# Layer-1 tables of the state-space branch: computed beside the layer-0 prompt attention instead of among the first projections

## The chip, the core and the metric

The kernel runs on one core of a Trainium2 chip. The metric is device time per execution in microseconds, as the median of the runs. Further numbers come from one execution that the hardware profiler recorded. The engines are TensorE (PE, matmuls; PEld is its weight loads), VectorE (DVE), ScalarE (ACT), GpSimd (POOL) and SyncE (SP, which issues all the DMAs here).

## What is computed

Two layers of a trunk with two parallel branches, for one prompt of 2048 tokens and eight samples of 16 tokens (each with 512 cached keys), width 1024. Cut from the reference:

```python
mod = silu(c) @ w_mod + b_mod                       # shift, scale, gate
h = rms_norm(x, norm_g) * (1 + scale) + shift
u, z_s, q, k, v, z_a = split(h @ w_in)              # each 512 wide
ab = exp((a_re + i a_im) * dt)                      # per group (32) and state (64)
bb = (ab - 1) / (a_re + i a_im) * b                 # input matrix
state_t = ab * state_{t-1} + bb @ u_t               # associative scan over time
y_s = Re(c @ state) + d_skip * u                    # then GELU and a half-GLU
z = q @ k.T / 8                                     # stick-breaking, s < t
a[t, s] = sigmoid(z[t, s]) * prod_{s<j<t} (1 - sigmoid(z[t, j]))
y_a = a @ v
x = x + gate * (concat(y_s * silu(z_s), y_a * silu(z_a)) @ w_out)
```

The state-space scan is not run token by token: chunks of 16 tokens are done by matmuls with matrices made of the powers of `ab`, and from chunk to chunk the state is carried by a scan in rotated coordinates. Those matrices and rotations depend on the weights alone. They are the tables that this document is about.

## The kernel before

Matmul operands of the projections are split into a high and a low part, so a product is three matmuls (hH wH, hH wL, hL wH). Tiles are 128 tokens; half 0 is tiles 0 to 7 and the samples' tile 16, half 1 is tiles 8 to 15. `build` (line 52 on) writes the work in this order: `mod` for layer 0 (conditioning), `ssm_params` (powers of `ab` for both layers, to DRAM), the projections of half 0 (`project`, first u and q, then k, v, za, zs), between them the tables, then half 1's projections with `ssm(0)` and `attn_sample(0)`, then `attn_prompt(0)`, `glu(0)`, the rest of `mod` (layer 0's gate and all of layer 1's), `output(0, 0)` (the output projection of half 0), and layer 1's projections.

The tables of a layer are made by two functions:

- `ssm_phase(l)` builds cos and sin of 128 chunk rotations by seven doublings. Each step multiplies on VectorE (lines 444, 447) and on GpSimd (445, 448) and joins on VectorE (446, 449); then `unit` normalises (ScalarE squares at 414 and 415, VectorE at 416 to 418, GpSimd at 419). The result T goes to DRAM (`ph_d`, 3 MB).
- `ssm_mats(l)` loads b, c and d, turns them by transposes on TensorE (497, 517), and makes in eight blocks of four groups EE (VectorE 551, GpSimd 550 and 552), GG (VectorE 556 and 557, GpSimd 555), KK (TensorE 563, ScalarE 566, VectorE 567) and mH (TensorE 573, ScalarE 576). The result goes to DRAM (`mm`, `kd`, `sm_d`; 10.5 MB).

`ssm(l)` and `ssm_sample(l)` read these tables from DRAM. Layer 0 needs its own early, in `ssm(0)`; layer 1 only in `ssm_sample(1)` and `ssm(1)`, which come after the layer-0 output.

`attn_prompt(l)` goes over blocks of four query tiles, pairs of heads and chunks of 512 keys. I call one such step a unit; layer 0 has 40, numbered from 0; the first chunk of each block and pair of heads is the masked one. In a unit TensorE makes scores (819, 820, and a mask at 822), ScalarE a sigmoid (824), VectorE a running product (826, shown as TENSOR_TENSOR_SCAN in the profile and as SCALAR_TENSOR_TENSOR in the program's order), TensorE transposes that (836), VectorE and ScalarE copy the transposes (838, 839) and TensorE multiplies with v (842). Up to 16 products `u` are kept, so the scores run about two units ahead.

SBUF is handed out as stacks from two sides. A pool that is opened where a closed one lay waits, tile by tile, until that tile's last user is done. On the right lie, one after another, the tables' pools, `ssm`, the sample attention and the prompt attention; on the left the projections' pool, then those of `glu`, `mod` and `output`. PSUM has tags: m (projections, `mod` on the left, output), z and t (scores and transposes of the attention, tables).

No order is written out by hand. At build time a scheduler goes over the program with a model of the engines and fixes a static order for each engine and for SyncE's queue; where several instructions are ready, the one written earlier goes first. On the chip each engine takes its instructions in that order and waits by semaphore, so an instruction that isn't ready holds all behind it on its engine.

Of the kernel before, what the change touches and what calls it, by code (L numbers as in the profile page):

```python
# [44 lines left out]
class Trunk:  # L45
# [6 lines left out]
    def build(self):  # L52
        tc, nc = self.tc, self.nc
        with ExitStack() as es:
            self.dram = es.enter_context(tc.tile_pool(name="dram", bufs=1, space=DRAM))
            self.cp = self.pool(es, "const")
            self.pes = ExitStack()
            self.mb, self.zb, self.tb, self.ob = 2, 2, 2, 1
            self.ps = self.pes.enter_context(tc.tile_pool(name="ps", bufs=1, space=PSUM))
            self.scratch()  # L60
            self.consts()
            with ExitStack() as pe:
                with ExitStack() as px:
                    self.xp, self.xf = self.pool(px, "xp", right=True), []
                    self.rs0 = self.xp.tile([128, NT], F32, name="rs")
                    self.fetch(0)
                    self.fetch(1)
                    with ExitStack() as pv:
                        su = self.pool(pv, "sv", right=True)
                        self.mod(0, (2, 3, 0, 1))  # L70
                        self.ssm_params(su)
                    st = self.proj_open(pe, 0, 0)
                    with tc.high_priority(offset=300):
                        self.project(st, ("u",))
                self.project(st, ('q',))
                with ExitStack() as pq:
                    self.stats(self.pool(pq, "stats1", right=True), TILES[1])
                self.ssm_mats(0)
                with ExitStack() as ph:
                    self.ssm_phase(ph, 0)  # L80
                    self.ssm_phase(ph, 1)
                self.ssm_mats(1)
                self.ssm_sample(0)
                self.project(st, ('k', 'v', 'za', 'zs'))
                self.proj_half(st, 1)
                self.project(st, ("u",))
                self.ssm(0)
                self.attn_sample(0)
                self.project(st, ('zs', 'za', 'k', 'v', 'q'))
            self.attn_prompt(0, ((0, 4), (4, 4), (8, 4), (12, 4)))  # L90
            self.glu(0)
            self.mod(0, (4, 5), right=False)
            self.mod(1, (2, 3, 0, 1, 4, 5), right=False)
            self.output(0, 0)
            with ExitStack() as pe:
                st = self.proj_open(pe, 1, 0)
                self.project(st, ("u",))
                self.project(st, ('q', 'k', 'v', 'za', 'zs'))
            self.attn_sample(1)
            self.output(0, 1)  # L100
            with ExitStack() as pe:
                st = self.proj_open(pe, 1, 1)
                self.project(st, ("u",))
                self.ssm_sample(1)
                self.ssm(1)
                self.project(st, ('k', 'v', 'q', 'zs', 'za'))
            self.pes.close()
            self.ps = es.enter_context(tc.tile_pool(name="ps2", bufs=1, space=PSUM))
            self.mb, self.zb, self.tb, self.ob = 1, 3, 3, 1
            self.attn_prompt(1, ((0, 4), (4, 4), (8, 4)) + ((12, 2), (14, 2)))  # L110
            self.glu(1)
            self.output(1, 0)
            self.output(1, 1)
# [304 lines left out]
        v.tensor_mul(c, c, t1)  # L418
        gp.tensor_mul(s, s, t1)

    def ssm_phase(self, es, l):
        v, gp = self.nc.vector, self.nc.gpsimd
        su = self.pool(es, f"sp{l}", right=True)
        pu = su.tile([128, 3, 16], F32, name="pu")
        self.dma(pu, self.pb_d[l][:, 1])
        T = su.tile([128, 2, 16, 128], F32, name="T")
# [26 lines left out]
        v.tensor_scalar(t1, s, -1.0, None, ALU.mult)  # L453
        self.dma(self.ph_d[l][:, 2], t1)

    def ssm_mats(self, l):
        nc, A = self.nc, self.A
        v, gp, ident = nc.vector, nc.gpsimd, self.ident
        NG = 4
        with ExitStack() as es:  # L460
            su = self.pool(es, f"sm{l}", right=True)
            PWT = su.tile([128, 18, 2, G], F32, name="PWT")
            self.dma(PWT, self.pw_d[l])
            FT = PWT[:, 17]
# [27 lines left out]
            C2 = su.tile([128, G, C], F32, name="C2")  # L492
            C3 = su.tile([128, G, C], F32, name="C3")
            for src, dst in ((Cn, C2), (Cm, C3)):
                ps = self.pt()
                for a in range(4):
                    nc.tensor.transpose(ps[:, a * 128:(a + 1) * 128], src[:, a, :, :].rearrange("p r x -> p (r x)"), ident)
                pv = ps.rearrange("p (g c) -> p g c", c=C)
# [13 lines left out]
            v.tensor_copy(ZB[hi, 1, :, 1], pairs(Bb1)[hi, :, 1])  # L512
            BT = su.tile([128, 2, 512], F32, name="BT")
            for r in range(2):
                ps = self.pt()
                for qt in range(4):
                    nc.tensor.transpose(ps[:, qt * 128:(qt + 1) * 128],
                                        ZB[:, r, qt * 4:(qt + 1) * 4].rearrange("p q g c -> p (q g c)"), ident)
                nc.scalar.copy(BT[:, r, :], ps)
# [22 lines left out]
            for b in range(G // NG):  # L542
# [13 lines left out]
                v.tensor_mul(GG, pw(0, 16), Bb1[:, gs].unsqueeze(2).to_broadcast([128, NG, 16, C]))  # L556
                v.tensor_add(GG, GG, t2)
                self.dma(self.mm[l][:, gs, 256:512], EE[:, :, 1:17, :].rearrange("p g n c -> p g (n c)"))
                ps = self.pz()
                for g in range(NG):  # L560
                    go = b * NG + g
                    lh = Bb1[:, go:go + 2, :] if go < G - 1 else Bz
# [5 lines left out]
                self.dma(self.kd[l][gs].rearrange("g c l k -> (g c) (l k)")[:, 256:512], KK)  # L568
                mH = su.tile([128, 2, NG, 128], F32, name="mH", bufs=2)
                for hf in range(2):  # L570
                    ps = self.pt()
                    for j in range(NG):
                        nc.tensor.transpose(ps[:, j * 128:(j + 1) * 128],
                                            GG[:, j, 8 - hf * 8:16 - hf * 8, :].rearrange("p t c -> p (t c)"), ident)
# [707 lines left out]
```

## Time and profile before

| | us |
|---|---|
| median of 3 runs (lowest, highest) | 3268.61 (3263.90, 3268.92) |
| the profiled execution | 3266.1 |
| its span, first to last instruction | 3264.3 |
| TensorE busy in the span | 3019.6 (93%) |
| VectorE busy | 2228.8 (68%) |
| ScalarE busy | 1297.2 (40%) |
| GpSimd busy | 715.0 (22%) |
| mean granted clock of TensorE | 0.971 |

Times in the trace count from the span's first instruction. A busy time is the union of an engine's instructions in a stretch. Ends of matmuls are modelled, so a busy TensorE may still hold some slack; how far apart matmuls start shows what one costs. A wait is put down to the instruction whose semaphore came last. The stretches used below are: 296 to 616 (both layers' phase tables, layer 1's matrices, and the k, v, za and zs projections of half 0), 1061 to 1383 (the layer-0 attention from the end of unit 0 to the end of unit 17), 1383 to 1914 (units 18 to 39).

### The profile page before, as it was taken

How to read it: one execution, taken by the hardware profiler on the slowest of the kernel's cores; microseconds unless marked ns; L12 is line 12 of the kernel's file. 1: busy time of each engine (PE TensorE's matmuls, PEld its weight loads, DVE VectorE, ACT ScalarE, POOL GpSimd, SP SyncE). 2: the span in 40 equal slices, each digit the busy share in tenths (PEclk: the TensorE clock that was granted, in tenths of full speed). 3: DMA queues.
4: the chain of work that ended last, by engine and by line, in shares of the span. 5: the costliest groups of instructions: out<-in, count | busy, mean ns of one | idle time of the engine just before them, and what ended most of it. 6: DMA issues, size and time to landing. Idle time of an engine off the chain costs nothing. (4 is left out here: it accounts for less than half of the span.)

```text
span 3264.3 us, 47172 instructions
## 1 busy us (share of the span) xinstructions
PE 3019.6 (93%) x16902; PEld 2241.4 (69%) x16902; DVE 2228.8 (68%) x3885; ACT 1297.2 (40%) x2646; POOL 715.0 (22%) x468
## 2 busy tenths in 40 slices
PE   6978679899998999999999999989999899999998
PEld 4756577798767667667777785757789565666665
DVE  6699785667466776677895534376583989776865
ACT  5622225334342343465443324263343345343422
POOL 1155663102211022211021002222200202111210
PEclk8989899999999999999999999999999899999999
DMA  6645654565776974343344237437853846444642
GB/s 208 164 141 176 215 166 150 146 192 167 258 241 216 315 218 151 121 139 117 113 150 153 88 104 268 142 99 216 268 177 119 259 129 200 141 128 136 203 140 73
DMA packets 516100, 555.28 MB, mean 170 GB/s; under 512 B 87203, under 2 KB 369491, under 8 KB 515098
## 3 DMA queue, kind: packets, MB, share of 16 engines
q1 hardware_dynamic: 515866, 552.26, 53.9%
q8 instruction: 134, 2.20, 0.3%
q14 instruction: 100, 0.82, 0.1%
HBM read 378.12 MB, written 169.86 MB: 168 GB/s over the span
## 5 line engine op out<-in xcount | busy, mean ns | idle before, releaser
L826 DVE TENSOR_TENSOR_SCAN u<-u 128x512 f32<-128x512 f32 (+3 forms) x640 | 722.2, 1162 | 94.2 <-ACT u L824 90.7
L673 PE MATMUL pm<-wH,hH 128*128 128x512 f32 x1088 | 448.9, 414 | 38.4 <-ACT kn L760 18.9
L675 PE MATMUL pm<-wH,hL 128*128 128x512 f32 x1088 | 446.2, 410 | 10.6 <-POOL hL L649 6.0
L674 PE MATMUL pm<-wL,hH 128*128 128x512 f32 x1088 | 444.0, 408 | 9.9 <-DVE wL L172 8.0
L839 ACT COPY aT<-pt 128x512 f32<-128x512 f32 (+1 forms) x376 | 174.9, 469 | 595.3 <-PE pt L836 569.1
L836 PEld LDWEIGHTS pt<-ident,u 128*128 128x128 f32 x2176 | 242.1, 142 | 230.8 <-issue 194.1
L824 ACT ACTIVATE u<-pz 128x512 f32<-128x512 f32 (+3 forms) x640 | 320.7, 535 | 177.1 <-PE pz L822 61.3
L838 DVE COPY aT<-pt 128x512 f32<-128x512 f32 (+1 forms) x376 | 199.4, 533 | 253.8 <-PE pt L836 242.3
L836 PE MATMUL pt<-ident,u 128*128 128x128 f32 x2176 | 352.0, 285 | 12.9 <-DVE aT L838 9.3
L842 PE MATMUL po<-aT,V 128*64 128x512 f32 (+1 forms) x1504 | 317.7, 505 | 16.0 <-DVE aT L838 8.1
L819 PE MATMUL pz<-K,Q 128*128 128x512 f32 (+2 forms) x640 | 272.9, 427 | 6.1 <-ACT u L824 1.8
L726 PE MATMUL pm<-hH,wH 128*128 128x384 f32 (+1 forms) x768 | 258.9, 337 | 18.4 <-DVE kn L731 18.4
L673 PEld LDWEIGHTS pm<-wH,hH 128*128 128x128 f32 x1088 | 210.0, 193 | 90.2 <-ACT kn L760 20.4
L728 PE MATMUL pm<-hH,wL 128*128 128x384 f32 (+1 forms) x768 | 257.4, 336 | 10.2 <-POOL wL L172 10.2
L172 POOL TENSOR_TENSOR wL<-wr,wH 128x512 fp32r<-128x512 f32 x96 | 152.1, 1595 | 498.2 <-ACT wH L171 326.8
L727 PE MATMUL pm<-hL,wH 128*128 128x384 f32 (+1 forms) x768 | 257.8, 336 | 0.0
L675 PEld LDWEIGHTS pm<-wH,hL 128*128 128x128 f32 x1088 | 210.2, 193 | 66.2 <-POOL hL L649 10.6
L674 PEld LDWEIGHTS pm<-wL,hH 128*128 128x128 f32 x1088 | 210.2, 193 | 58.8 <-DVE wL L172 11.3
L820 PE MATMUL pz<-K,Q 128*128 128x512 f32 (+2 forms) x640 | 236.3, 370 | 0.0
L1241 PE MATMUL pm<-owH,mH 128*128 128x512 f32 x512 | 205.0, 402 | 2.1 <-ACT mH L171 1.2
L1242 PE MATMUL pm<-owL,mH 128*128 128x512 f32 x512 | 204.1, 399 | 3.1 <-DVE owL L172 3.1
L1243 PE MATMUL pm<-owH,mL 128*128 128x512 f32 x512 | 202.4, 396 | 0.0
(373 smaller groups left out, 5252.0 us busy)
## 6 DMA issues: line engine op xcount, KB each, us to landing
wr<-in_w_in_dram SPq DMA_DIRECT2D x192, 256.0 KB
K<-kT SPq DMA_DIRECT2D x184, 256.0 KB
Q<-qT SPq DMA_DIRECT2D x112, 256.0 KB
wm<-in_w_mod_dram SPq DMA_DIRECT2D x24, 1024.0 KB
V<-dv_d SPq DMA_DIRECT2D x92, 256.0 KB
out_dram<-kn SPq DMA_DIRECT2D x68, 256.0 KB
qT<-x SPq DMA_DIRECT2D x64, 256.0 KB
kT<-x SPq DMA_DIRECT2D x64, 256.0 KB
```

The lines of the kernel that those rows point to most:

```text
L673: pe.matmul(ps, hH[:, k, cs], wH[k], start=k == 0, stop=False)
L674: pe.matmul(ps, hH[:, k, cs], wL[k], start=False, stop=False)
L675: pe.matmul(ps, hL[:, k, cs], wH[k], start=False, stop=k == KT - 1)
L726: pe.matmul(ps[:, 0:n], wH[k][:, ws], hH[:, k, 0:n], start=k == 0, stop=False)
L727: pe.matmul(ps[:, 0:n], wH[k][:, ws], hL[:, k, 0:n], start=False, stop=False)
L728: pe.matmul(ps[:, 0:n], wL[k][:, ws], hH[:, k, 0:n], start=False, stop=k == KT - 1)
L819: pe.matmul(pz[:, c0:512], Q1[:, qi], K1[:, 0:N], start=True, stop=False)
L820: pe.matmul(pz[:, c0:512], Q2[:, qi], K1[:, 0:N], start=False, stop=not diag)
L824: sc.activation(u[:, o:512], pz[:, c0:c1], AF.Sigmoid, scale=-0.125)
L826: v.tensor_tensor_scan(un, un, un, 1.0 if diag else carry[hh * 4 + i], ALU.mult, ALU.bypass)
L836: pe.transpose(pTs[hh][:, i * 128:(i + 1) * 128], As[hh][i][:, off + j * 128:off + (j + 1) * 128], ident)
L842: mm = pe.matmul(po[c, s], V1[:, j, c], aTs[hh][:, s], start=diag and j == 0, stop=kc == 0 and j == 3, tile_position=(0, hh * 64))
```

## The change

The two calls for layer 1 leave the place behind layer 0's tables and go behind `glu(0)`, on the left side of SBUF: `ssm_phase(1)` in one scope with the remaining `mod` calls, `ssm_mats(1)` after them and before `output(0, 0)`. In the left form `ssm_mats` takes its PSUM tiles from tag m instead of z and t. Instructions and operands are the same; layer 0 keeps the right side.

```diff
                     self.ssm_phase(ph, 0)
-                    self.ssm_phase(ph, 1)
-                self.ssm_mats(1)
                 self.ssm_sample(0)
...
             self.glu(0)
-            self.mod(0, (4, 5), right=False)
-            self.mod(1, (2, 3, 0, 1, 4, 5), right=False)
+            with ExitStack() as ph:
+                self.ssm_phase(ph, 1, right=False)
+                self.mod(0, (4, 5), right=False)
+                self.mod(1, (2, 3, 0, 1, 4, 5), right=False)
+            self.ssm_mats(1, right=False)
             self.output(0, 0)
...
-    def ssm_phase(self, es, l):
+    def ssm_phase(self, es, l, right=True):
...
-        su = self.pool(es, f"sp{l}", right=True)
+        su = self.pool(es, f"sp{l}", right=right)
...
-    def ssm_mats(self, l):
+    def ssm_mats(self, l, right=True):
         nc, A = self.nc, self.A
+        pt, pz = (self.pt, self.pz) if right else (self.pm, self.pm)
...
-            su = self.pool(es, f"sm{l}", right=True)
+            su = self.pool(es, f"sm{l}", right=right)
...
-                ps = self.pt()
+                ps = pt()
...
-                ps = self.pz()
+                ps = pz()
```

Since the scheduler decides, the order of the engines shows more than the diff. Line numbers of the changed kernel are higher by one from `glu` in `build` on and by two from `ssm_mats` on.

First place: VectorE beside the za and zs projections of half 0 (kn is their gated tile, L731 before and L733 after; wL a low weight part). Before, among them stand the layer-1 matrices:

```order
L551 TENSOR_TENSOR EE<-PWT,C_2489 128x1088
L556 TENSOR_TENSOR GG<-PWT,Bb_2474 128x1024
L567 TENSOR_TENSOR KK<-KK,Dd 128x16
L731 TENSOR_TENSOR kn<-pm,kn 128x384
L557 TENSOR_TENSOR GG<-GG,Gt 128x1024
L551 TENSOR_TENSOR EE<-PWT,C_2489 128x1088
L731 TENSOR_TENSOR kn<-pm,kn 128x384
```

After, the state recurrence of `ssm_sample(0)` (HS, sta, stb) stands there:

```order
L733 TENSOR_TENSOR kn<-pm,kn 128x384
L1130 TENSOR_TENSOR sta<-HS,a_2403 128x256
L1131 TENSOR_TENSOR stb<-HS,a_2403 128x256
L1132 TENSOR_TENSOR HS<-HS,sta 128x256
L1133 TENSOR_TENSOR HS<-HS,stb 128x256
```

The matrices left this place, and the sample recurrence, which stood behind them, moved up into it.

Second place: TensorE in the attention, unit 11 of the order before and unit 13 of the order after. Before, the matmuls of `output(0, 0)` (owH, owL, mH, mL) stand between the attention's scores:

```order
L820 MATMUL pz<-K_10660,Q_10648 128x512
L822 LDWEIGHTS identb
L822 MATMUL pz<-maskb,identb 128x128
L1242 MATMUL pm<-owL_14875,mH 128x512
L1243 MATMUL pm<-owH_14874,mL 128x512
L1241 MATMUL pm<-owH_14876,mH 128x512
L1242 MATMUL pm<-owL_14877,mH 128x512
L1243 MATMUL pm<-owH_14876,mL 128x512
```

After, the transposes and small matmuls of `ssm_mats(1)` (GG, EE; L575 and L565) stand there, and the attention's own:

```order
L575 MATMUL pm<-ident,GG 128x128 x8
L844 MATMUL po<-aT,V_10230 64x128 x2
L838 MATMUL pt<-ident,u 128x128 x4
L565 MATMUL pm<-EE,Bb_14507 32x256 x4
L838 MATMUL pt<-ident,u 128x128 x4
L844 MATMUL po<-aT,V_10344 64x512 x2
L838 MATMUL pt<-ident,u 128x128 x8
```

The first matmul of `output(0, 0)` moved from unit 10 to unit 18, and all of its 432 with it.

Third place: VectorE in the attention, unit 11 before and unit 15 after (u is the scan, aT the copied transposes). Before, splits of output's weights and activations (owL, mL) stand among them:

```order
L826 SCALAR_TENSOR_TENSOR u<-u 128x512
L838 COPY aT<-pt 128x512
L172 TENSOR_TENSOR mL<-m,mH 128x512
L826 SCALAR_TENSOR_TENSOR u<-u 128x512 x2
L851 SCALAR_TENSOR_TENSOR za<-po,vE,za 128x128 x4
L838 COPY aT<-pt 128x384
```

After, the blocks of the layer-1 matrices:

```order
L828 SCALAR_TENSOR_TENSOR u<-u 128x512 x2
L840 COPY aT<-pt 128x512
L558 TENSOR_TENSOR GG<-PWT,Bb_14507 128x1024
L553 TENSOR_TENSOR EE<-PWT,C_14522 128x1088
L569 TENSOR_TENSOR KK<-KK,Dd 128x16
L840 COPY aT<-pt 128x512
L559 TENSOR_TENSOR GG<-GG,Gt 128x1024
```

The phase table of layer 1 stands in the same way among units 3 to 8, and on SyncE's queue the matrices' writes stand between the attention's K and V loads.

## Rows read from the trace of the kernel before

Names are those of the program with buffer numbers left out. Shapes are out<-in.

**Rows 1.** Stretches: busy PE, PEld, DVE, ACT, POOL (instructions); PEclk, DMA share, GB/s.
```profile
296.00:616.00 320.00, 253.85 (x1340) 214.45 (x1341) 240.13 (x307) 109.25 (x204) 164.53 (x95) 0.94 0.52 165
1061.00:1198.00 137.00, 132.30 (x1079) 82.81 (x1080) 98.93 (x160) 55.20 (x118) 9.79 (x5) 0.96 0.86 269
1198.00:1383.00 185.00, 185.00 (x934) 130.40 (x933) 120.82 (x165) 71.83 (x141) 50.31 (x32) 1.00 0.47 151
1383.00:1914.00 531.00, 522.62 (x2724) 376.52 (x2722) 378.26 (x652) 244.96 (x469) 77.27 (x51) 1.00 0.38 121
2550.00:2800.00 250.00, 229.76 (x1235) 155.52 (x1235) 215.85 (x259) 105.27 (x217) 42.24 (x19) 0.95 0.62 183
```

**Rows 2.** TensorE's waits, 296 to 616: waiter, releaser, us in all, times, longest.
```profile
PE pm L673 <- ACT kn L760: 18.6, 3, 9.3
PE pm L726 <- DVE kn L731: 16.8, 6, 5.3
PE pm L728 <- POOL wL L172: 7.9, 2, 4.0
PE pt L573 <- DVE GG L557: 6.4, 3, 2.9
```

**Rows 3.** Two projection matmuls in the timeline: start, us, engine, line, tiles.
```profile
1568.06 0.40 PE L675 MATMUL pm<-wH,hL 128*128 128x512 f32 x1
1568.29 0.40 PE L673 MATMUL pm<-wH,hH 128*128 128x512 f32 x1
```

**Rows 4.** TensorE's groups, 296 to 616: count, busy us, mean ns, idle before.
```profile
L726 PE MATMUL pm<-hH,wH 128*128 128x384 f32 x200 | 71.9, 359 | 16.8 <-DVE kn L731 16.8
...
L673 PE MATMUL pm<-wH,hH 128*128 128x512 f32 x134 | 56.0, 419 | 24.1 <-ACT kn L760 18.6 <-DVE hH L648 4.7 <-ACT kn L686 0.8
```

**Rows 5.** ScalarE's squares of the phase tables, group of 296 to 395.5.
```profile
L414 ACT ACTIVATE t<-T 128x2048 f32<-128x2048 f32 x2 | 3.8, 1910 | 14.8 <-DVE T L449 14.8
```

**Rows 6.** VectorE's groups of output(0, 0), by shape, 1061 to 1383.
```profile
L172 DVE TENSOR_TENSOR mL<-m,mH 128x512 fp32r<-128x512 f32 x9 | 11.1, 1235 | 0.5 <-issue 0.3 <-ACT mH L171 0.2
L1244 DVE TENSOR_TENSOR yt<-pm,gpr 128x512 f32<-128x512 f32 x16 | 10.8, 675 | 1.5 <-issue 1.4
...
L172 DVE TENSOR_TENSOR owL<-owr,owH 128x512 fp32r<-128x512 f32 x8 | 7.0, 891 | 0.7 <-ACT owH L171 0.7
```

**Rows 7.** VectorE's largest phase-table group, both layers, 296 to 395.5.
```profile
L416 DVE TENSOR_TENSOR t<-t,t 128x2048 f32<-128x2048 f32 x2 | 9.0, 4496 | 1.6 <-ACT t L415 1.6
```

**Rows 8.** VectorE's groups of the layer-1 matrices, 396 to 520.
```profile
L556 DVE TENSOR_TENSOR GG<-PWT,Bb 128x1024 f32<-128x1024 f32 x8 | 17.5, 2193 | 4.4 <-PE pt L573 4.4
L551 DVE TENSOR_TENSOR EE<-PWT,C 128x1088 f32<-128x1088 f32 x8 | 13.6, 1706 | 4.3 <-DMA mm<-EE 4.3
...
L567 DVE TENSOR_TENSOR KK<-KK,Dd 128x16 f32<-128x16 f32 x8 | 10.2, 1274 | 0.0
```

**Rows 9.** TensorE's group of one output line, 1061 to 1383.
```profile
L1241 PE MATMUL pm<-owH,mH 128*128 128x512 f32 x144 | 56.3, 392 | 0.0
```

**Rows 10.** VectorE's 512-column scans, 1098 to 1150, 1200 to 1250; then both stretches.
```profile
L826 DVE TENSOR_TENSOR_SCAN u<-u 128x512 f32<-128x512 f32 x18 | 22.1, 1260 | 1.4 <-ACT u L824 1.4
...
L826 DVE TENSOR_TENSOR_SCAN u<-u 128x512 f32<-128x512 f32 x13 | 19.1, 1501 | 1.5 <-ACT u L824 1.5
...
1098.00:1150.00 52.00, 52.00 (x466) 32.52 (x464) 34.69 (x56) 17.69 (x37) 0.00 (x0) 1.00 1.04 334
1200.00:1250.00 50.00, 50.00 (x255) 35.15 (x252) 37.93 (x49) 21.81 (x44) 19.44 (x11) 1.00 0.55 179
```

**Rows 11.** SyncE's DMA queue, waits from 396 to 520.
```profile
SPq L163 <- DVE KK L567: 20.7, 7, 7.8
```

**Rows 12.** GpSimd's groups of the layer-1 matrices, 396 to 516.
```profile
L552 POOL TENSOR_TENSOR EE<-EE,Et 128x1088 f32<-128x1088 f32 x8 | 24.3, 3033 | 2.3 <-issue 1.9
L550 POOL TENSOR_TENSOR Et<-PWT,C 128x1088 f32<-128x1088 f32 x8 | 19.6, 2454 | 0.7 <-DVE C L503 0.6
L555 POOL TENSOR_TENSOR Gt<-PWT,Bb 128x1024 f32<-128x1024 f32 x8 | 18.7, 2334 | 33.2 <-DVE Bb L483 15.9 <-DVE GG L557 13.7 <-DVE KK L567 3.5
```

More of the change, by code (lines that the diff above doesn't have):

```diff
@@ L514, in ssm_mats @@
             for r in range(2):
-                ps = self.pt()
+                ps = pt()
                 for qt in range(4):
@@ L570, in ssm_mats @@
                 for hf in range(2):
-                    ps = self.pt()
+                    ps = pt()
                     for j in range(NG):
```

## The prediction

> **What bounds the kernel now.** First I read the busy time by stretch [rows 1]. TensorE is the engine that the end waits for: beside the layer-0 prompt attention and the projections behind it, from 1383 to 1914, it is busy 522.6 of 531 us, so a matmul that is put there makes the kernel longer by its own length. Two stretches are of another kind. From 296 to 616, where both layers' tables (ssm_phase and ssm_mats) stand beside the k, v, za and zs projections, TensorE is busy 253.9 of 320 us and its granted clock is 0.94, which is a mix of its two levels of 1.2 and 2.4 GHz; GpSimd has 164.5 us of work there, more per us than in any other of these stretches. From 1061 to 1383, the attention's units 1 to 17 (a unit is four query tiles by two heads by 512 keys; layer 0 has 40), TensorE is full too, but not by attention alone: the whole of output(0, 0) stands between.
>
> Next come TensorE's waits in the early stretch, by what ended them [rows 2]. Of 66.3 us in all, 49.7 are in four groups: 18.6 for the copy of a v tile out of PSUM, 16.8 for VectorE's za/zs multiply, 7.9 for a GpSimd weight split, 6.4 for the tables' own GG. VectorE's multiply and the splits are short; they come late because the tables' instructions stand ahead of them on engines that work in order.
>
> Last, the unit prices. Two 512-column matmuls of the projections start 0.23 us apart where nothing waits [rows 3]; I take 0.17 for 384 columns, three quarters of it.
>
> **What is removed early, and what that gives.** The change takes the layer-1 tables out of the early stretch. TensorE's work there is 404 matmuls at 0.23 (92.9 us), 598 at 0.17 (102) [rows 4], the 112 instructions of the layer-1 tables (most of them 128 columns wide, which I put at 9 us in all) and some 20 us of transposes and sample work: 224 us in a stretch of 320. So the gain can't exceed 96 us of waiting and slow clock plus these 9. What of it hangs on the layer-1 tables? The GG wait, 6.4, whole. The waits for the multiply, 16.8, whole: in the new order VectorE has the layer-0 sample recurrence beside za and zs in place of EE and GG, in instructions a quarter as long. Of the v copies, two waits of some 9 us each carry 18.6: in one GpSimd itself waits for the v tile's round trip through DRAM, which stays; in the other ScalarE had a square of the phase table ahead of the copy, and that waited 14.8 us for both layers' phase recurrences taking turns [rows 5], so 9.3 goes. Of the weight splits half, 4. That is 36.5. Of the clock, 0.06 times 320 is 19 us lost, and I count 15 as returned, since the clock falls behind idle time. With the 9 us of tables the early gain is **60 us**. The bounds: 25, if only the waits on GG, the v copy and the 9 us come back; 95, if nearly all does.
>
> **What the tables cost beside the attention.** They now stand on VectorE and GpSimd among units 3 to 18. VectorE is busy 98.9 + 120.8 = 219.8 us from 1061 to 1383 [rows 1], of which 30.3 belong to output(0, 0): 11.1 + 7.0 for its splits, 10.8 for its gating and 1.4 for the gating's small second group, by [rows 6]. Attention, glu and mod alone are 189.4. The phase table of one layer adds half of what both take early: its largest group is that in [rows 7], 9.0 us for two layers, and with the 35 others it comes to 72 us for two layers, so 36 (26 where GpSimd doesn't stretch them). The matrices add 17.5 + 13.6 + 10.2 and 10.8 for the GG sums plus 17 for 24 small set-up groups of 0.1 to 2.6 us, 69 us as they ran early [rows 8], and some 46 where each runs at its undisturbed length (1.2 to 1.3 us for GG and EE against 2.2 and 1.7 in the rows). Together VectorE has 261 to 294 us; I take 278, between.
>
> How much time does that need? VectorE is in order, each scan waits for a ScalarE sigmoid and each copy for TensorE's transposes, so it is never full there. The nearest row is the layer-1 attention with glu's VectorE work beside it, 2550 to 2800: 215.9 of 250 us, 0.86 [rows 1]. At 0.87 the 278 us need **320 us**: as long as now (322). The bounds are 261, VectorE full and undisturbed, and 360.
>
> **What moves behind.** The pool of output(0, 0) takes the left memory that the layer-1 matrices hold, so its weights load after them: in the new order its first matmul stands at unit 18, where it stood at unit 10. Its 432 matmuls (144 of each of three lines, [rows 9]) ran inside the stretch of 322 us; now the stretch takes as long without them, and TensorE idles there for about 100 us. At 0.23 they are **99 us**, and they run where TensorE is full already [rows 1], each pushing a projection matmul out behind the attention. Nothing is late there to hide them. The 9 us of table matmuls fall into TensorE's new idle time and cost nothing; if VectorE turned out to be no bound, they would cost those 9.
>
> DMAs: 3 MB of phase table and 10.5 MB of matrices are written later. The DMA share is 0.86 from 1061 to 1198 and 0.47 from 1198 to 1383 [rows 1], so the bytes fit, but for mod's weights around 1100, where the share is 1.04 at 334 GB/s [rows 10]: 3 MB there are 9 us, inside the upper bound. What costs more is the place in SyncE's queue. Early, seven KK writes made that queue wait 20.7 us [rows 11]; now K and V loads of the attention stand behind such writes, with three K and two V buffers. That is inside the upper bound of 360.
>
> **The sum**, against the profiled execution's own 3266.1 us (span 3264.3 and 1.8 around it): -60 early, -2 in the attention's stretch, +99 behind it. 3303 us. The median of the runs is 2.5 above the profiled one, less than I can resolve here, so I leave the sum at **3303**.
>
> **A rule that speaks against overlap.** A 512-column scan, which reads SBUF twice, takes 1260 ns from 1098 to 1150, where GpSimd does nothing, and 1501 from 1200 to 1250, with GpSimd busy 19.4 of 50 us [rows 10]. So the two engines disturb each other, in part. The Trainium skill ("SBUF — State Buffer", Who interferes with whom) says that a VectorE instruction with two SBUF inputs and a GpSimd instruction that reads SBUF don't share the port: the second "fully blocks". By that rule the time would be the second rival's; by the rows it lies between that and the sum above.
>
> **Rivals.** (1) *The tables fit into VectorE's idle time, and the kernel gets faster.* VectorE is idle 38 of 137 and 64 of 185 us in the stretch now. If attention's waits and the tables interleave so well that 272 us of work take 275 us, and the early stretch gives 85, the sum is 3266 - 85 - 47 + 99 = 3233. It decides from the point where the early gain and the shortening of the stretch together pass 105 us. For it: the early waits add up to more than I count, and VectorE's idle is there. Against: the nearest stretch has VectorE at 0.86 [rows 1], and here ScalarE, TensorE and GpSimd all stand between its instructions. 0.17.
> (2) *VectorE and GpSimd exclude each other beside the attention, or K and V loads come late.* GpSimd's layer-1 matrices are 24.3 + 19.6 + 18.7 = 62.6 us [rows 12] and its phase part some 19. Added to VectorE's 278 in place of running beside it, the stretch is 360: 3266 - 60 + 38 + 99 = 3343. Against: from 396 to 516 both engines ran these tables and together were busy longer than the time that passed. 0.16.
> (3) *The change doesn't do early what it says, or gains and losses cancel.* If the early stretch is held by DMA round trips and by the layer-0 tables that remain, it gives 25 and the sum is 3336, which is inside (2)'s range and counted with it. If it gives 75 and the stretch takes 298, the sum is 3266 - 75 - 24 + 99 = 3266: no change. 0.11.
>
> **Numbers.** The forecast, 3275 to 3332, has 0.56; (2) 0.16; (3) 0.11; (1) 0.17. A measurement of this kernel can tell about 0.2% (6.5 us) from no change. Slower: 0.56 + 0.16 = 0.72; same 0.11; faster 0.17. The range runs from 3250, which takes in (3) and the nearer part of (1), to 3345, which takes in (2); about 0.1 is left out on each side.
>
> **What would show it.** Right: from 296 on, the waits for the za/zs multiply and for GG are gone and zs ends some 40 us sooner; the attention's units 1 to 17 take about 320 us with TensorE busy some 215 of them; output(0, 0) starts only behind them; the attention's end is close to where it was, and some 100 us more of projections stand behind it without attention. Wrong early: TensorE still waits for v copies and weight splits from 296 to 616. Wrong beside the attention: units 1 to 17 take 280 us or less (the forecast falls, towards faster), or scans and GpSimd's products take half as long again as now and the stretch takes 350 (rival 2). If output's matmuls come in before unit 17's end, the 99 us were counted too high.

## The result, and the profile after

The changed kernel takes 3313.78 us (median of 4 runs, 3307.21 to 3319.65), the kernel before in the same series 3266.26 (3259.15 to 3268.92): a ratio of 1.0148, 95% interval 1.0122 to 1.0174. The profiled execution took 3313.76 us with a span of 3312.0. The forecast was 3303, in a range from 3250 to 3345.

Five stages show where it went. A unit ends with its last transpose; unit 40 is the first of the layer-1 attention, so the fourth column holds what stands between the two attentions: output, the layer-1 projections and the sample work. "Displaced" counts the matmuls of output and projections that stand behind unit 39 by the program's order and stood ahead of its end in the kernel before. Stages are from the profiled execution of each kernel, in us; the labels are those of the experiments below.

| kernel | to the end of unit 0 | units 1 to 17 | units 18 to 39 | to the end of unit 40 | rest | displaced | median |
|---|---|---|---|---|---|---|---|
| before | 1061 | 322 | 531 | 625 | 725 | 0 | 3266 |
| after | 1001 | 320 | 524 | 747 | 720 | 544 | 3314 |
| e1, no layer-1 tables | 993 | 299 | 532 | 663 | 717 | 177 | 3215 |
| e4, matrices moved alone | 1016 | 313 | 517 | 754 | 722 | 584 | 3326 |
| e5, phase table moved alone | 1058 | 326 | 523 | 654 | 723 | 144 | 3286 |
| e3, output first | 995 | 331 | 505 | 748 | 722 | 568 | 3307 |
| e6, VectorE's products out | 997 | 291 | 527 | 737 | 719 | 531 | 3277 |
| e7, GpSimd's products out | 995 | 282 | 524 | 745 | 723 | 536 | 3271 |
| e9, all products on VectorE | 993 | 303 | 516 | 757 | 724 | 584 | 3296 |
| e10, before, all on VectorE | 1059 | 301 | 533 | 662 | 725 | 177 | 3279 |
| e2, both tables behind the attention | 1000 | 303 | 533 | 739 | 712 | 177 | 3287 |
| e8, matrices behind the attention | 998 | 334 | 512 | 700 | 725 | 147 | 3270 |
| e11, e8 with all on VectorE | 996 | 335 | 510 | 763 | 690 | 147 | 3296 |
| e12, matrices spread over output(0, 1) | 996 | 332 | 511 | 726 | 724 | 147 | 3299 |

So the change gains 60 us early and loses 122 behind the attention; the other stages give back 14. Busy time by stretch of the changed kernel, with the columns of [rows 1]: the early stretch, units 1 to about 8, units 9 to 17, units 18 to 39, and the part up to unit 40.

```profile
296.00:556.00 260.00, 227.44 (x1179) 198.06 (x1178) 125.49 (x214) 91.86 (x173) 71.95 (x53) 0.95 0.46 150
1001.00:1147.00 146.00, 136.18 (x1096) 85.80 (x1094) 121.04 (x199) 55.77 (x114) 19.49 (x16) 0.96 0.80 258
1147.00:1321.00 174.00, 126.74 (x642) 71.12 (x640) 164.43 (x163) 62.03 (x125) 73.90 (x27) 0.81 0.50 146
1321.00:1845.00 524.00, 516.39 (x2609) 359.89 (x2607) 398.07 (x686) 251.09 (x479) 98.34 (x67) 0.99 0.40 129
1845.00:2592.00 747.00, 703.15 (x3885) 564.90 (x3883) 358.80 (x726) 260.80 (x533) 141.10 (x112) 0.97 0.54 173
```

The same of the kernel before, from the end of unit 39 to that of unit 40:

```profile
1914.00:2539.00 625.00, 588.74 (x3342) 463.56 (x3340) 340.65 (x705) 241.09 (x496) 117.40 (x95) 0.98 0.58 184
```

TensorE has 543 more matmuls there and needs 122 us more. From 1147 to 1321, beside the layer-1 matrices, VectorE is busy 164.4 of 174 us: that is where the bound has changed. TensorE is idle 47 us of it and its granted clock is 0.81, so it was at the lower of its two levels for part of the stretch. Its waits there (waiter, releaser, us in all, times, longest) are for VectorE's copies:

```profile
PE po L844 <- DVE aT L840: 20.2, 9, 5.2
PE pt L838 <- DVE aT L840: 16.3, 5, 8.9
```

The early waits that answer to [rows 2] (the copy of a v tile; the za/zs multiply) are, from 296 to 556 of the changed kernel:

```profile
PE pm L675 <- ACT kn L762: 11.4, 2, 8.1
PE pm L728 <- DVE kn L733: 8.3, 4, 3.5
```

### The profile page after: what moved, and what is told of

It reads as the page before. It is cut to its first block, busy times and chain, and to the rows that moved or that the text cites. A ratio compares the mean times of both kernels' runs of the same rounds, so it can differ in the third digit from the quotient of the medians.

```text
span 3312.0 us, 47127 instructions
## 1 busy us (share of the span) xinstructions
PE 3045.3 (92%) x16902; PEld 2249.3 (68%) x16902; DVE 2223.3 (67%) x3885; ACT 1299.3 (39%) x2646; POOL 704.2 (21%) x468
## 4 chain that ended last, share of the span: by engine, by line
PE 48%; DVE 8%; DMA 3%; issue 2%; ACT 1%; SPq 0%; POOL 0%; DVEq 0%; ACTq 0%; POOLq 0%
PE pt L838 6%; PE po L844 6%; PE pm L1243 3%; PE pm L1244 3%; PE pm L1245 3%; DVE u L828 3%; PE pm L677 3%; PE pm L676 3%; PE pm L675 3%; PE pz L821 3%; PE pz L822 2%; PE pm L728 2%; PE pm L730 2%; PE pm L729 2%; PE pz L893 1%
## 5 line engine op out<-in xcount | busy, mean ns | idle before, releaser
L828 DVE TENSOR_TENSOR_SCAN u<-u 128x512 f32<-128x512 f32 (+3 forms) x640 | 746.5, 1199 | 77.4 <-ACT u L826 74.4
L838 PE MATMUL pt<-ident,u 128*128 128x128 f32 x2176 | 364.1, 289 | 33.7 <-DVE aT L840 27.3
L844 PE MATMUL po<-aT,V 128*64 128x512 f32 (+1 forms) x1504 | 325.4, 516 | 40.8 <-DVE aT L840 29.1
```

Source lines behind the costliest of these rows:

```text
L828: v.tensor_tensor_scan(un, un, un, 1.0 if diag else carry[hh * 4 + i], ALU.mult, ALU.bypass)
L838: pe.transpose(pTs[hh][:, i * 128:(i + 1) * 128], As[hh][i][:, off + j * 128:off + (j + 1) * 128], ident)
L844: mm = pe.matmul(po[c, s], V1[:, j, c], aTs[hh][:, s], start=diag and j == 0, stop=kc == 0 and j == 3, tile_position=(0, hh * 64))
```

## Experiments

All are edits of the changed kernel, except where another base is named.

**Without the tables.** What does the early stretch give if nothing is paid later?

```diff
-                self.ssm_phase(ph, 1, right=False)
...
-            self.ssm_mats(1, right=False)
...
+        for t in (self.ph_d, self.sm_d, self.kd, self.mm):
+            t[1] = t[0]
```

> The layer-1 tables are left out altogether; layer 1 reads those of layer 0, so its numbers are other ones. Everything else is the changed kernel. My reading (the early stretch gains 60 us, and the whole loss comes from the tables standing beside the attention): unit 0 ends near 1000 as in the changed kernel, nothing is displaced for good, 3266 - 60 = 3206 us, 3195 to 3215. Rival (part of the early gain is given back later whatever stands beside the attention, since another chain sets the end there): 3225 to 3250.

3215.31 us, ratio 0.9848 (0.9824 to 0.9872), at the upper edge of the expected range. The early gain is 68 us at the end of unit 0. In the profiled execution 60 us are left of it at the end, by the medians 49: the layer-1 tables cost some 50 us where the kernel before has them. Busy time for units 1 to 17, 18 to 39, and up to unit 40:

```profile
993.00:1292.00 299.00, 291.71 (x1893) 189.54 (x1892) 215.92 (x294) 123.94 (x250) 41.13 (x28) 0.99 0.66 208
1292.00:1824.00 532.00, 522.39 (x2677) 370.42 (x2674) 380.49 (x672) 243.01 (x463) 81.42 (x54) 0.99 0.39 124
1824.00:2488.00 664.00, 620.49 (x3519) 493.31 (x3517) 348.91 (x721) 249.27 (x511) 125.15 (x99) 0.98 0.56 176
```

TensorE is full (0.98) in units 1 to 17, as before. 177 matmuls are displaced here too, which lengthens the fourth stage by 38 us, but 23 come back as shorter units 1 to 17 and 8 in the last stage. A displaced matmul is a loss only if the place that it left does not get shorter.

**The two parts apart.** e4 leaves the phase table early, e5 the matrices:

```diff
                     self.ssm_phase(ph, 0)
+                    self.ssm_phase(ph, 1)
...
-                self.ssm_phase(ph, 1, right=False)
```

> Only the layer-1 matrices are moved; its phase table stays early. By the terms of the prediction the matrices carry the waits on GG (6.4), on the za/zs multiply (16.8) and the weight splits (4), the 9 us of table matmuls and most of the clock: early gain 45, against 15 for the phase table. In its order 584 matmuls are displaced behind the attention (at 0.225 us 131), and without the phase table units 1 to 17 have 258 us of VectorE work, at 0.87 297 us instead of 322. Sum: 3266 - 45 - 25 + 131 - 13 (units 18 to 39 and the rest, as in the changed kernel) = 3314, 3300 to 3325. Rival (the phase table has the larger part of the early gain, since the v copies and multiplies wait for its recurrence): early gain 20, 3335 to 3345.

```diff
                     self.ssm_phase(ph, 0)
+                self.ssm_mats(1)
...
-            self.ssm_mats(1, right=False)
```

> The counterpart of the run with the matrices alone: only the phase table of layer 1 is moved, the matrices stay early. If the two parts add up, the early gain is 60 - 45 = 15 us (unit 0 ends at 1046), and the phase table costs 7 to 9 us in units 1 to 17, where TensorE stays the bound (between the changed kernel and the one with the matrices alone these units differ by 7 us, and TensorE is 0.93 busy in the part where the phase table stands): 3266 - 15 + 8 = 3259, 3252 to 3264. Rival (the phase table, too, pushes output out from beside the attention: 144 matmuls by its order, 32 us): 3280 to 3292.

Matrices alone: 3326.05 us, ratio 1.0188 (1.0168 to 1.0208). Phase table alone: 3285.64, ratio 1.0068 (1.0054 to 1.0081). In e4 the early gain is 45, as expected, but units 1 to 17 take 313, not 297, and the time lies just over the expected range. In e5 the early gain is 3, not 15, and the fourth stage is 29 us longer with 144 displaced: the rival of that run. TensorE's early waits of e4, then of e5:

```profile
PE pm L675 <- ACT kn L762: 18.7, 3, 9.3
PE pm L730 <- POOL wL L173: 8.5, 2, 4.4
PE pm L728 <- DVE kn L733: 6.8, 3, 3.6
```

```profile
PE pm L728 <- DVE kn L733: 22.6, 4, 11.6
PE pm L675 <- ACT kn L762: 12.2, 2, 7.8
PE pt L575 <- DVE GG L559: 6.4, 3, 2.7
```

With the phase table early, the v copies and the weight split stay late (18.6 and 7.9 in [rows 2]); without it the v copies lose 6.4 us, so it was the phase table that held them (by my reading its squares on ScalarE). The multiply waits for the matrices: 16.8 before, 6.8 without them. In e5 it is 22.6 with one wait of 11.6, which takes back what the v copies give: so 45 and 3 make 60 only together.

**Output ahead of the matrices.**

```diff
+            self.output(0, 0)
             self.ssm_mats(1, right=False)
-            self.output(0, 0)
```

> output(0,0) is written ahead of the layer-1 matrices, both still on the left. In this order output's matmuls stand at units 10 to 18 as in the kernel before, the matrices at units 21 to 25, and no layer-1 projection between units 19 and 27, where there are some 430 in the kernel before; in all 568 matmuls of output and projections stand behind the attention that stood beside it before (544 in the changed kernel). My reading (whatever comes behind the matrices on the left is displaced, it needn't be output): as the changed kernel, 3314 us, 3300 to 3325. Rival (it was output(0,0) that lost its cover, and the later units have room on VectorE for the matrices): 3230 to 3260.

3306.98 us, ratio 1.0143 (1.0115 to 1.017), the same as the changed kernel. Output has its old place, now the projections lose theirs; units 18 to 39 get 26 us shorter than before and the fourth stage 123 longer. It is not output that matters, but that the matrices stand ahead of whatever fills TensorE. In the changed kernel output's first weight loads (owr) leave SyncE's queue right behind the last write of the matrices (start, us, engine):

```profile
1304.99 0.98 SPq L164 DMA_DIRECT2D mm<-mH  x2
1306.03 2.11 SPq L164 DMA_DIRECT2D owr<-in_w_out_dram  x4
```

In e3 the projections' first weight loads follow the last write in the same way, at 1497.8 behind 1497.3. That it is the left memory that holds them, and not the written order alone, I read from the pools; no run separates the two.

**Which engine's products cost it?** In the layer-1 matrices e6 leaves out VectorE's, e7 GpSimd's:

```diff
-                v.tensor_mul(EE, pw(0, 17), ...)
-                gp.tensor_add(EE, EE, t1)
+                if l == 0:
+                    v.tensor_mul(EE, pw(0, 17), ...)
+                gp.tensor_add(EE, EE if l == 0 else t1, t1)
...
+                if l == 1:
+                    t2 = GG
...
-                v.tensor_mul(GG, pw(0, 16), ...)
-                v.tensor_add(GG, GG, t2)
+                if l == 0:
+                    v.tensor_mul(GG, pw(0, 16), ...)
+                    v.tensor_add(GG, GG, t2)
```

> Left out: VectorE's 24 products and sums of EE and GG in the layer-1 matrices (GpSimd's 24 stay, each writing in place), so layer 1's tables are wrong; all else is the changed kernel. If VectorE is the bound beside the matrices (0.945 busy in 174 us), its 46 to 58 us less there shorten units 1 to 17 by about 45, to 275, and TensorE's clock comes back from 0.81: 3314 - 45 = 3269, 3258 to 3280. Rival (VectorE's work fits in, what costs is the wait of TensorE's transposes and of the DMA queue behind the tables' results): units 1 to 17 stay over 305 us, 3295 to 3314.

```diff
-                gp.tensor_mul(t1, pw(1, 17), ...)
+                if l == 0:
+                    gp.tensor_mul(t1, pw(1, 17), ...)
...
-                gp.tensor_add(EE, EE, t1)
+                if l == 0:
+                    gp.tensor_add(EE, EE, t1)
...
-                gp.tensor_mul(t2, pw(1, 16), ...)
+                if l == 0:
+                    gp.tensor_mul(t2, pw(1, 16), ...)
...
-                v.tensor_add(GG, GG, t2)
+                v.tensor_add(GG, GG, t2 if l == 0 else GG)
```

> Left out: GpSimd's 24 products and sums of EE and GG in the layer-1 matrices (VectorE's 24 stay), so layer 1's tables are wrong; all else is the changed kernel. My reading (VectorE's own work is the bound, GpSimd only stretches some of it): VectorE's instructions of the matrices fall from 2.2 and 1.7 us to 1.2 or 1.3, some 15 us in all, units 1 to 17 take 300 to 308: 3314 - 15 = 3299, 3290 to 3308. Rival (the two engines exclude each other, so GpSimd's 62 us are paid in full by VectorE): units 1 to 17 take 265 to 280, 3255 to 3275.

e6: 3277.49 us, ratio 1.0051 (1.0032 to 1.0069). e7: 3271.3, ratio 1.0033 (1.0019 to 1.0046). Units 9 to 17 of e6, then of e7, with the same columns:

```profile
1143.00:1288.00 145.00, 117.44 (x651) 67.16 (x650) 132.81 (x139) 65.63 (x133) 68.36 (x30) 0.92 0.66 192
```

```profile
1141.00:1277.00 136.00, 114.67 (x651) 66.30 (x650) 125.66 (x164) 62.50 (x130) 6.74 (x5) 0.92 0.70 201
```

In both VectorE stays at 0.92 of the stretch, and the stretch shortens with VectorE's busy time: 164.4 to 132.8 with e6, to 125.7 with e7. That it is the bound there holds. What I did not expect is that taking away GpSimd's instructions helps VectorE more than taking away its own. 67 us less on GpSimd are 39 less on VectorE (I had put 15). So e6 took the time that I expected, though its units 1 to 17 took 291 us and not 275, and e7 lies in the range of its rival, at 39 us for GpSimd's work and not the full 62. VectorE's groups beside the matrices, of the changed kernel (count, busy us, mean ns, idle before):

```profile
L828 DVE TENSOR_TENSOR_SCAN u<-u 128x512 f32<-128x512 f32 x47 | 74.3, 1607 | 0.0
L840 DVE COPY aT<-pt 128x512 f32<-128x512 f32 x23 | 15.5, 672 | 5.0 <-PE pt L838 5.0
L558 DVE TENSOR_TENSOR GG<-PWT,Bb 128x1024 f32<-128x1024 f32 x8 | 14.9, 1863 | 1.8 <-PE pm L575 1.8
L569 DVE TENSOR_TENSOR KK<-KK,Dd 128x16 f32<-128x16 f32 x8 | 4.9, 617 | 0.0
L528 DVE COPY ZC<-C 64x256 f32<-64x256 f32 x1 | 2.5, 2541 | 0.0
```

and of e7:

```profile
L831 DVE TENSOR_TENSOR_SCAN u<-u 128x512 f32<-128x512 f32 x46 | 58.9, 1305 | 0.0
L843 DVE COPY aT<-pt 128x512 f32<-128x512 f32 x23 | 15.5, 676 | 4.2 <-PE pt L841 4.2
L561 DVE TENSOR_TENSOR GG<-PWT,Bb 128x1024 f32<-128x1024 f32 x8 | 9.6, 1206 | 0.6 <-PE pm L578 0.6
L572 DVE TENSOR_TENSOR KK<-KK,Dd 128x16 f32<-128x16 f32 x8 | 1.3, 158 | 0.0
L528 DVE COPY ZC<-C 64x256 f32<-64x256 f32 x1 | 0.3, 291 | 0.0
```

The copies out of PSUM take the same; scans and products, which read SBUF twice, don't. Nor do five small set-up instructions from SBUF to SBUF with one input, of which the last line is one: 2.0 to 2.5 us each beside GpSimd, 0.3 without it, some 10 of the 39 us.

**All products on VectorE.** e9 does in the changed kernel, and e10 in the kernel before for both layers, what GpSimd did for EE and GG on VectorE. What is computed stays the same.

```diff
-                gp.tensor_mul(t1, pw(1, 17), ...)
+                (v if l == 1 else gp).tensor_mul(t1, pw(1, 17), ...)
...
-                gp.tensor_add(EE, EE, t1)
+                (v if l == 1 else gp).tensor_add(EE, EE, t1)
...
-                gp.tensor_mul(t2, pw(1, 16), ...)
+                (v if l == 1 else gp).tensor_mul(t2, pw(1, 16), ...)
```

> The changed kernel, with GpSimd's 24 products and sums of EE and GG in the layer-1 matrices done by VectorE instead; the result is the same. Without them VectorE was 125.7 us busy beside the matrices (164.4 with them on GpSimd); 24 more of some 1.23 us make 155 us, at a share of 0.93 167 us in place of 174: units 1 to 17 take 313 us, 3314 - 7 = 3307, 3297 to 3313. Rival (the stretching by GpSimd was no fixed price for its work, and taking over its work costs VectorE more than it got back): 3318 to 3335.

> The kernel before, with GpSimd's products and sums of EE and GG of both layers' matrices done by VectorE. Early, VectorE's instructions of one layer's matrices took 17.5 + 13.6 + 10.8 + 10.2 = 52 us beside GpSimd and take some 31 without it; 24 more of 1.23 are 30: 9 us more of VectorE work for each layer, but no chain from engine to engine in a block and 62 us less of GpSimd ahead of the weight splits. My reading: within 10 us of before, 3253 to 3272. Rival (the GpSimd part is what makes the tables' early place dear): 3235 to 3250.

e9: 3296.49 us, ratio 1.0111 (1.0094 to 1.0128), 17 us under the changed kernel (12 by the two ratios) and just under the expected range, with units 1 to 17 at 303. Beside the matrices:

```profile
1139.00:1296.00 157.00, 122.49 (x656) 67.70 (x653) 151.73 (x187) 60.91 (x125) 2.71 (x2) 0.87 0.52 152
```

```profile
L828 DVE TENSOR_TENSOR_SCAN u<-u 128x512 f32<-128x512 f32 x48 | 59.4, 1259 | 0.0
L558 DVE TENSOR_TENSOR GG<-PWT,Bb 128x1024 f32<-128x1024 f32 x8 | 9.7, 1209 | 0.6 <-PE pm L575 0.6
```

VectorE does 24 more instructions and is still busy 12.7 us less than with GpSimd's help. e10: 3279.03 us, ratio 1.0052 (1.0036 to 1.0068), over both expected ranges. Early it gains 2 us, so at that place the exchange is about even, as I had read it; the 17 us lost lie in an attention order with 177 matmuls displaced, the same counts as in e1, which my expectation had left out.

**The matrices behind the attention.** e2 puts both tables on the right behind the first layer-1 projections; e8 only the matrices, with a lower priority asked for; e11 is e8 with all products on VectorE; e12 ties each block of the matrices to a tile of output(0, 1).

```diff
-                self.ssm_phase(ph, 1, right=False)
...
-            self.ssm_mats(1, right=False)
...
+            with ExitStack() as ph:
+                self.ssm_phase(ph, 1)
+            self.ssm_mats(1)
             self.attn_sample(1)
```

> The layer-1 tables are written behind the layer-0 output and the first layer-1 projections, ahead of the layer-1 sample attention, on the right side of memory and with the PSUM tags of the attention, so they can start when the layer-0 attention is done. My reading (the loss beside the attention is that TensorE has no other work there; behind it the projections are there, and VectorE is busy 91 of 236 us): early gain 60, about 9 us of table matmuls on a full TensorE: 3215 us, 3205 to 3230. Rival (the tables hold up projections wherever they stand beside them, as they did from 296 to 616): the 60 us are lost again, 3260 to 3275.

```diff
-            self.ssm_mats(1, right=False)
...
+            with tc.high_priority(offset=-1500):
+                self.ssm_mats(1)
             self.attn_sample(1)
```

> The phase table stays where the changed kernel has it; the matrices are written behind the first layer-1 projections, ahead of the layer-1 sample attention, on the right side and with PSUM tags z and t. Without the phase table in front they start right when the layer-0 attention is done, beside 200 projection matmuls that are left. If what cost 76 us in the run with both tables late was mainly the matrices in one dense group (TensorE waits in order for GG, and K and za loads for KK writes): 3206 + 9 (phase) + 9 + 40 to 50 = 3264 to 3274. Rival (it was the phase table's recurrence that delayed them into a stretch with nothing else for TensorE): 3215 to 3240, which would beat both kernels.

> The kernel with the late matrices (phase table as in the changed kernel), with GpSimd's products and sums in the layer-1 matrices done by VectorE. If GpSimd's share is what stretches the matrices in their dense group there, the wait of TensorE for GG falls: 3270 - 10 to 20 = 3250 to 3260. Rival (the dense group in order is the cost, whoever does it): 3265 to 3275.

```diff
-            self.ssm_mats(1, right=False)
...
-            self.attn_sample(1)
-            self.output(0, 1)
+            with ExitStack() as ms:
+                steps = self.ssm_mats_steps(ms, 1)
+                next(steps)
+                self.attn_sample(1)
+                self.output(0, 1, hook=steps)
...
+                if hook:
+                    self.pace = mm
+                    next(hook, None)
```

> Phase table as in the changed kernel; the eight blocks of the layer-1 matrices are on the right side, each held by a dependency until TensorE is done with the matmuls of the next tile of output(0,1), so one block stands beside each of the eight tiles (48 matmuls, some 11 us) in place of one dense group. If the tables are dear because they come dense while TensorE has nothing else in its order, they cost here little more than their own matmuls: 3206 + 9 (phase table) + 9 + 5 to 20 = 3229 to 3244, which beats both kernels. Rival (in-order waits for GG, and loads behind KK writes on the DMA queue, cost the same however they are spread): 3262 to 3280.

e2: 3286.76 us, 1.0068 (1.005 to 1.0086). e8: 3270.31, 1.0024 (1.0014 to 1.0034). e11: 3296.18, 1.011 (1.0092 to 1.0129). e12: 3299.12, 1.0108 (1.0091 to 1.0126). None beats the kernel before; e8 lies in its expected range, the other three lie over both of theirs. In e2 the fourth stage takes 739 us, 76 more than in e1. Two stretches of it, the waits of TensorE in the stage, and one of the DMA queue (1836 to 2140):

```profile
1900.00:1960.00 60.00, 32.16 (x159) 26.24 (x158) 49.59 (x43) 14.62 (x28) 37.94 (x16) 0.71 0.77 214
1960.00:2020.00 60.00, 48.46 (x199) 36.78 (x200) 45.01 (x29) 15.72 (x29) 52.64 (x25) 0.81 0.48 153
```

```profile
PE pt L576 <- DVE GG L560: 27.6, 7, 13.3
PE pz L822 <- DMA za<-za_d: 14.1, 1, 14.1
```

```profile
SPq L165 <- DVE KK L570: 35.8, 7, 8.6
```

The eight blocks come in one dense group; the transposes of GG stand in TensorE's queue ahead of the rest and wait for VectorE, and the granted clock is lower there (0.71 and 0.81). The room on VectorE was there, but the order did not spread the work over it. The wait of 14.1 us is another matter: it ends at 2560, before the first scores of layer 1, some 500 us behind the matrices. DMA writes did wait for KK in SyncE's queue (35.8 us), but that a load which TensorE needed stood behind them is not shown. e8 pays less there: it has no phase table in that stage, its group starts 26 us behind the attention's end and not 78, GG waits are 19.8 us up to unit 40, and the stage takes 700 us. In e11 the wait for GG from 1841 to 2200 is 0.4 us, so the local reading held, but the sample attention starts at 2056 in place of 1997 and the fourth stage takes 763 us; 35 us come back in the last stage. The run does not tell what GpSimd costs there. In e12 the blocks are spread as meant, but output(0, 1) starts behind the sample attention, its matmuls at 2005 to 2124 where e1 has 1925 to 2057:

```profile
1980.00:2040.00 60.00, 39.15 (x228) 26.91 (x227) 30.36 (x31) 19.54 (x35) 27.11 (x17) 0.82 0.50 157
2100.00:2160.00 60.00, 36.66 (x181) 26.83 (x180) 36.28 (x49) 21.60 (x36) 44.44 (x21) 0.77 0.62 203
```

Whether a place exists where the tables cost less than the some 50 us of their old one stays open.

## Why the prediction was right, point by point

**Early, -60: measured -60, with terms that were off both ways.** TensorE's idle time in the stretch fell from 66.2 us [rows 1] to 32.6, 33.6 against 36.5 forecast. GG's 6.4 are gone as counted. The multiply gave 8.5 in place of 16.8 (16.8 to 8.3), the v copies 7.2 against 9.3, the weight splits nearly all of 7.9 against 4; the rest is in small groups. Busy time fell by 26.4, where 24 were forecast, but otherwise divided: the tables had 144 matmuls and not 112, 64 of them 256 columns wide, and 17 us, not 9, which these groups of the kernel before show (296 to 616; the other four have 2.8 us):

```profile
L573 PE MATMUL pt<-ident,GG 128*128 128x128 f32 x64 | 9.3, 282 | 6.4 <-DVE GG L557 6.4
L563 PE MATMUL pz<-EE,Bb 128*32 128x256 f32 x62 | 5.1, 391 | 0.1
```

So some 9 us are left, where I counted 15 for the clock; some 3 of them are 17 projection matmuls fewer between the edges of the stretch, which leaves 6 for the clock. That the terms add up to 60 is luck. The last za/zs multiply of half 0 ends at 510 in place of 542, 32 us sooner where I had said some 40.

**Units 1 to 17, 320: measured 320, partly by luck.** VectorE was busy 285.5 us against 278 and filled 0.89 of the stages against 0.87. But one share over the whole stretch is the wrong picture. Where the phase table stands TensorE is the bound (136.2 of 146 us), and only beside the matrices is it VectorE (0.945). By my rule e4, with 258 us of VectorE work, should have taken 297; it took 313. Without the phase table its part of the stages is only 12 us shorter (134 for 146), though 28 us of VectorE's work are gone from it, so most of that work had not been on the path:

```profile
1016.00:1150.00 134.00, 130.27 (x1064) 81.91 (x1063) 92.92 (x152) 49.24 (x106) 0.95 (x1) 0.99 0.77 245
```

Also wrong: TensorE was busy 263 us in these units, not 215; the clock was at 0.81 in part of them and the tables' 17 us of matmuls stand there too. And VectorE can be nearly full beside the attention, which I had ruled out.

**Behind the attention, +99: the mechanism right, the size too small.** I counted output's 432 matmuls. 544 were displaced: behind output there is a gap until the layer-1 projections can start (64 matmuls in units 16 to 18 before, 36 in units 25 to 27 after, against 143 to 198 in their neighbours), and it had moved with output into the units that should hold the projections. The price was right: 122 us for 544 are 0.224 each, and 0.20 to 0.23 follows from the fourth stage of e1, e3, e4, e5, e9 and e10 in the same way. Units 18 to 39 gave 7 us back and the rest 5, so the term was 110 net, and this is the 11 us between forecast and span (+47.7 where the sum said +37). My remark that the attention's end would stay where it was contradicted my own sum: it came 69 us earlier.

**Rival 1 (it fits).** It needed early gain and shortening to pass 105 us; they came to 62: 60 early where it wanted 85, and 2 in the stretch where it wanted 47. The second fell because of the 0.945 of VectorE beside the matrices.

**Rival 2 (VectorE and GpSimd exclude each other).** Its time, 3343, was not reached, but its mechanism is there, and I weighed it wrongly. From means over 50 us [rows 10] I took the disturbance as partial. And what I set against the rival, that both engines together were busy longer than the time that passed, proves nothing: an instruction that is held counts as busy. Two stretches of the timeline of the changed kernel (start, us, engine), first VectorE, then GpSimd, show it instruction by instruction:

```profile
1231.37 0.16 DVE L569 TENSOR_TENSOR KK<-KK,Dd 128x16 f32<-128x16 f32 x1
...
1244.19 2.00 DVE L569 TENSOR_TENSOR KK<-KK,Dd 128x16 f32<-128x16 f32 x1
...
1247.57 2.87 DVE L828 TENSOR_TENSOR_SCAN u<-u 128x512 f32<-128x512 f32 x1
```

```profile
1243.15 3.02 POOL L557 TENSOR_TENSOR Gt<-PWT,Bb 128x1024 f32<-128x1024 f32 x1 [3.79 <-DVE GG L559]
1246.13 3.22 POOL L554 TENSOR_TENSOR EE<-EE,Et 128x1088 f32<-128x1088 f32 x1
```

A sum of 16 columns takes 0.16 us at 1231 and 2.00 at 1244, where it ends with GpSimd's product (1246.17) and not before. The scan at 1247.57 takes 2.87 us: up to the end of GpSimd's sum at 1249.35, and then 1.09. The Trainium skill ("SBUF — State Buffer", Who interferes with whom) says that a VectorE instruction with two SBUF inputs contends with a GpSimd instruction that reads SBUF, that the shared port pair is "an exclusive lock", and that issue order decides which of them blocks; these rows agree, and so do the PSUM copies that are not disturbed (672 and 676 ns). My mean hid this, because only some scans are held. Of the 47 beside the matrices 37 take 1.26 us (six of these overlap a GpSimd instruction, four having begun before it), and ten take 2.2 to 3.5; each of the ten ends 1.08 or 1.09 us after the end of the GpSimd instruction that was running when it began. The 1501 ns of [rows 10] are of the same kind: 9 of its 13 scans take 1.25 us and 4 were held. The price per us of GpSimd work here is 0.58 of VectorE (39 of 67), not 1, and part of it was already inside my 278 us, which lies 17 over the undisturbed 261.

The other half of this rival did not come. SyncE's queue waited longer for KK beside the attention than the 20.7 us early (1147 to 1321):

```profile
SPq L164 <- DVE KK L569: 38.6, 7, 9.0
```

Yet from 1001 to 1321 TensorE's matmuls waited only 0.4 us in all for K and V loads.

**Rival 3 (gains and losses cancel)** would have needed units 1 to 17 at 298. e1 has 299, but without any tables. (Its other form, an early gain of 25, adds up to 3338 by my own terms and not to 3336.)

## What to carry to other kernels

If work is moved beside a stage that TensorE fills with two kinds of matmuls, ask first what the moved work keeps from starting, by the memory that it holds or by its place in the program, and count every matmul that then has to stand alone, the ones behind it too; here each cost its start distance of 0.22 us, less what the stage it left got shorter. Look for the bound in the part of a stage where the moved work really stands, not over the whole stage. Where VectorE is the bound, GpSimd's help is paid for by VectorE: here three GpSimd instructions a block cost it more than doing them itself.

## What the runs showed that was not expected

GpSimd's products and sums delay VectorE's instructions with two SBUF operands until the running GpSimd instruction ends, whatever their size (KK's sum: 158 ns alone, up to 2.0 us), and five set-up instructions of one SBUF operand too (0.3 alone, 2.0 to 2.5 us). A stretch in which TensorE waits much also had a lower granted clock: 0.81 beside the matrices (busy 126.7 of 174 us), 0.71 and 0.81 in e2, 0.77 in e12, against 0.99 for units 1 to 17 without the tables (291.7 of 299).
